# Attention: the first key block's product ahead of the third block's transposes, and where the projection passes stand

## The chip, the cores and the metric

The kernel runs on one core of a Trainium2 chip. The measured number is device time in microseconds (us) of one execution; smaller is better. The engines are TensorE (PE in the profile, its weight loads PEld), VectorE (DVE), ScalarE (ACT), GpSimd (POOL) and SyncE (SP, which issues the transfers).

## The reference, cut to what matters

One encoder layer over 1024 rows of width 1024. The mixing half has sliding-window attention (8 query heads, 2 key/value heads, blocks of 128 queries that see three blocks of 128 keys) beside a retention branch; both go through one output projection, and a gated feed-forward follows. The part that the change touches is the attention:

```python
s = einsum('bnqkgd,bnjkd->bnkgqj', qb, kb) * scale      # 128 queries x up to 3x128 keys
p = exp(s - m) / (sum(exp(s - m)) + exp(sink - m))      # m: row maximum, with the sink
o = einsum('bnkgqj,bnjkd->bnqkgd', p, vb)               # o: the product with the values
h = x + concat(o, retention) @ w_out
```

## The kernel before

Everything is float32. Each operand of a large product is split into a rounded part (hi, type fp32r) and the remainder (lo), and a product is three passes: hi by hi, hi by lo, lo by hi. A pass is one matmul of 128x512.

The attention stage is a loop of 16 steps (`for i in range(2 * NT)`, L782): query block t from 0 to 7, and key/value head kv 0 and 1. The generator `attend(t, kv, ...)` (L665) makes one step; its tiles are named after it, so `q40p` is a tile p of block 4, head 0. In it, four head rows j:

- scores: two matmuls for each j into a PSUM bank (`s`), then one VectorE instruction adds the mask and takes the extremum (`sm`, `nm`). `es` is a VectorE addition of 128x4 for the sink.
- ScalarE takes the exponentials (`sm`, sums into `den`). VectorE adds `es` to `den` and takes the reciprocal; then GpSimd and ScalarE, two rows each, scale `sm` (table entry `p_n`).
- transposes: for each key block b of nb (3; for t = 0 and 7 only 2), four 128x128 transposes of `sm` into a bank `p` on TensorE. ScalarE copies the bank to `ph` (hi), VectorE subtracts to `pl` (lo: bank `p` minus `ph`).
- product: for each b one matmul with `ph` and one with `pl` into bank `o`. ScalarE and VectorE add the two halves of `o` into `yA`.
- after head 1, GpSimd writes the block's rows to `X_hi` and `X_lo` (table entries `o_h`, `o_l`), from where the output projection reads them.

Transposes and products stand in two loops over b: all transposes first, then all products. `ph` has two buffers (tag t2), so the third `ph` is written once the first product has read the first. The banks come from five auxiliary ones (`AX_BUFS`), which the scores, the transposes and `o` share.

Beside these steps run, in the same loop, the queries of later blocks (`query`, tiles `q`, `q_t`, `qs`, `pt`, `qT`), the transposes of the retention rows (`ret_rows`, tiles `py`, `yw`), and projection passes that need nothing of the current step. `fill(n)` (L292) emits round(3n) passes from a fixed sequence, as long as their operands and a bank are there: first the rest of the query projection (tiles `d`), then the output projection (tiles `o`, whose weights `wh`, `wl` are split by GpSimd or ScalarE and VectorE on the way). The table `FILL` (L38) holds the counts; `fill(FILL["T1"])` at L699 emits 9 passes ahead of the transposes of each step.

The order of the code is not the order on the engines. A scheduler sorts each engine's instructions by readiness and priority as it computes them; program order decides between equals, and buffers set the waits. So a change of the emission order in `attend` changes the order on TensorE, and with it that of VectorE, ScalarE and GpSimd through the whole attention stage.

Of the kernel before, what the change touches and what calls it, by code (L numbers as in the profile page):

```python
# [34 lines left out]
       "r_bqh": "a", "r_bql": "ad", "r_sh": "a", "r_sl": "d", "r_y": "d", "r_sq": "a", "r_yn": "p", "r_yg": "p",  # L35
       "q_rope": "d", "k_rope": "d", "q_n": "d", "q_h": "p", "q_l": "dp", "q_T": "a", "p_n": "apap", "p_h": "a",
       "o_c": "a", "o_h": "p", "o_l": "p", "y_h": "a", "m_h": "da"}
FILL = {"A": 2, "Aend": 7, "B1": 2, "B2": 5, "C1": 4, "C2": 4, "D0": 6, "D1": 2, "T1": 3, "O0": 4, "O1": 4, "O2": 3}  # L38
SOONER = {"w": -80, "exp": 10, "pass": 0}
EARLY, LATE = (0, 4, 1, 5), (2, 3, 6, 7)  # L40
LEAD = 6
# [21 lines left out]
def hymba_block(ctx, tc, x, xT, cst, prm, ffnw, wqkv, wkv, wout, wg, wu, wd, out):  # L63
# [37 lines left out]
    def on(op, i=0):  # L101

        e = ENG[op]
        return {"a": act, "d": dve, "p": pool}[e[i % len(e)]]

    def copy(op, out, in_, i=0, scale=None):

        eng = on(op, i)
        if eng is act:
            act.activation(out, in_, AF.Copy, scale=1.0 if scale is None else scale)  # L110
        elif scale is not None:
            eng.tensor_scalar(out, in_, scale, 1.0, op0=ALU.mult, op1=ALU.mult)
        elif eng is dve:
            dve.tensor_copy(out, in_)
        else:
            pool.tensor_scalar(out, in_, 1.0, 1.0, op0=ALU.mult, op1=ALU.mult)
# [16 lines left out]
    def f32(ap):  # L133
        return ap.bitcast(F32)

    def U(name, tag, dt=F32):
        return up.tile([P, 512], dt, name=name, tag=tag, bufs=SLOTS[tag])
# [4 lines left out]
    def ax_ps(name):  # L142
        return pp.tile([P, 512], F32, name=name, tag="ax", bufs=AX_BUFS)
# [8 lines left out]
    def x_rows(t, k0):  # L152

        return tuple(X[:, k0:k0 + 4, t * P:t * P + P] for X in (X_hi, X_lo))

    def four(v):
        return v[:].rearrange("p (j n) -> p j n", n=P)
# [34 lines left out]
    A, B, C, D, O = "a", "b", "c", "d", "o"  # L192
# [57 lines left out]
    def sip():  # L250

        c, t, k = seq[pos[0]]
        per = 2 if c[0] == C else 1
        g = first_granule[c] + k // per
        i = part[0]
        if i == 0:
            while len(W) <= g:
                load_next()
            if c == chunks[0] and t == 0:
                split_x(k, 0)  # L260
            if k == 0:
                banks[c, t] = (ax_ps if c == chunks[0] and t in EXTRA else mm_ps)(f"{c[0]}{c[1]}_{t}")
                begun[0] += 1
        width = 512 // per
        o = (k % per) * width
        lh, ll = (X[:, k, t * P:t * P + P] for X in (X_hi, X_lo))
        rh, rl = (w[:, o:o + width] for w in W[g])
        with sooner("pass"):
            pe.matmul(banks[c, t][:, :width], ll if i == 2 else lh, rl if i == 1 else rh,
                      start=k == 0 and i == 0, stop=k == 7 and i == 2)  # L270
        part[0] = (i + 1) % 3
        if i < 2:
            return
        pos[0] += 1
        if c == chunks[0] and t == 3:
            split_x(k, 1)
        if k == 7:
            done.add((c, t))
        if t == tiles[c][-1] and (k + 1) % per == 0:
            freed[0] = g + 1  # L280
        if not hold[0] and pos[0] % PUMP == 0:
            pump(1)

    def ready():
        if pos[0] >= len(seq):
            return False
        c, t, k = seq[pos[0]]
        if (c[0], t, k // 4) in blocked:
            return False
        return k > 0 or part[0] > 0 or begun[0] - taken[0] < MM_BUFS + (len(EXTRA) if c == chunks[0] else 0)  # L290

    def fill(n):  # L292

        n = round(3 * n)
        while n and ready():
            sip()
            n -= 1
# [138 lines left out]
    def kv_scan(g, KV):  # L436
        gg = bc(gt[:, :, 2 * g:2 * g + 2], 3, HD)
        for s in range(1, 7):
            tmp = st.tile([P, 2, 2, HD], F32, name=f"sc{g}{s}", tag="sc", bufs=1)
            on("scan").tensor_tensor(tmp[:], KV(s - 1), gg, op=ALU.mult)  # L440
            on("scan").tensor_tensor(KV(s), KV(s), tmp[:], op=ALU.add)
# [83 lines left out]
    def drain(gen):  # L525
        for _ in gen:
            pass

    def go(gen):
        next(gen, None)  # L530
# [4 lines left out]
    for g in range(2):  # L535
# [4 lines left out]
        for t in range(NT):  # L540
# [9 lines left out]
            drain(prev)  # L550
            fill(FILL["A"])
            go(gen)
# [8 lines left out]
        drain(prev)  # L561
        fill(FILL["Aend"])
        kv_scan(g, KV)
        vhl = U(f"vhl{g}0", TAG["vhl"], F32R)
        states(g, 0, KV, BD, krv[0][:, 256:512], vhl)
        for c in range(NT):
# [6 lines left out]
            go(old)  # L573
            fill(FILL["B1"])
            go(gen)
            drain(old)
            fill(FILL["B2"])
            go(gen)
# [86 lines left out]
    def attend(t, kv, qT, yA):  # L665


        n = f"q{t}{kv}"
        b0 = max(t - 1, 0)
        nb = min(t + 1, NT - 1) - b0 + 1  # L670
        nk = nb * P
        mo = (b0 - (t - 1)) * P
        hs = slice(4 * kv, 4 * kv + 4)
        nm, es, den = (st.tile([P, 4], F32, name=f"{n}{v}", tag=v) for v in ("nm", "es", "den"))
        pr = []
        for j in range(4):
            pss = ax_ps(f"{n}s{j}")
            for i in range(2):
                pe.matmul(pss[:, :nk], qT[kv][:, j * P:j * P + P], K[:, 2 * kv + i, b0 * P:b0 * P + nk],
                          start=i == 0, stop=i == 1)  # L680
            sm = U(f"{n}sm{j}", "kr")
            dve.tensor_tensor_reduce(sm[:, :nk], pss[:, :nk], mask[:, mo:mo + nk], 1.0, 3.0e38, ALU.add, ALU.min,
                                     accum_out=nm[:, j:j + 1])
            pr.append(sm)
        dve.tensor_tensor(nm[:], nm[:], nsink[:, hs], op=ALU.min)
        dve.tensor_tensor(es[:], nm[:], sink[:, hs], op=ALU.add)
        yield
        for j in range(4):
            act.activation(pr[j][:, :nk], pr[j][:, :nk], AF.Exp, bias=nm[:, j:j + 1], scale=-1.0,
                           accum_out=den[:, j:j + 1])  # L690
            if j == 0:
                act.activation(es[:], es[:], AF.Exp)
        yield
        dve.tensor_tensor(den[:], den[:], es[:], op=ALU.add)
        dve.reciprocal(den[:], den[:])
        for j in range(4):
            copy("p_n", pr[j][:, :nk], pr[j][:, :nk], j, den[:, j:j + 1])
        yield
        fill(FILL["T1"])  # L699
        po = ax_ps(f"{n}o")  # L700
        ph, pl = [], []
        for b in range(nb):
            pt = ax_ps(f"{n}p{b}")
            for j in range(4):
                pe.transpose(pt[:, j * P:j * P + P], pr[j][:, b * P:b * P + P], f32(ident[:]))
            ph.append(U(f"{n}ph{b}", TAG["ph"], F32R))
            pl.append(U(f"{n}pl{b}", TAG["pl"], F32R))
            copy("p_h", ph[b][:], pt[:], b)
            dve.tensor_tensor(pl[b][:], pt[:], f32(ph[b][:]), op=ALU.subtract)
        for b in range(nb):  # L710
            vv = vview(b0 + b)[:, kv].rearrange("p i e -> p (i e)")
            pe.matmul(po[:], vv, ph[b][:], start=b == 0, stop=False)
            pe.matmul(po[:], vv, pl[b][:], start=False, stop=b == nb - 1)
        yield
        own = slice(kv * HD, kv * HD + HD)
        other = slice(HD - kv * HD, P - kv * HD)
        copy("o_c", yA[own, :], po[other, :])
        dve.tensor_tensor(yA[own, :], yA[own, :], po[own, :], op=ALU.add)
        if kv:
            yh, yl = x_rows(t, 0)  # L720
            copy("o_h", yh, four(yA))
            on("o_l").tensor_tensor(yl, four(yA), f32(yh), op=ALU.subtract)
            blocked.discard((O, t, 0))
# [14 lines left out]
    for t in range(NT):  # L738
# [6 lines left out]
        drain(old)  # L745
        fill(FILL["C1"])
        drain(prev)
# [171 lines left out]
    def prepare(n):  # L919

        for unit, v in order[prepared[0]:prepared[0] + n]:
            if v == "A11":
                for w in ("A11", "A12", "A21", "A22"):
                    block(unit, w)
            ready_ops[unit, v] = split(f"{v}_{unit[0]}{unit[1]}", block(unit, v))
        prepared[0] += n
# [6 lines left out]
    def product(ps, unit, v, xv, first, last):  # L933
        prepare(max(0, used[0] + 1 + LEAD - prepared[0]))
        used[0] += 1
        wh, wl = ready_ops[unit, v]
        xh, xl = XOP[xv]
        for k in range(4):
            c = slice(k * P, k * P + P)
            passes(ps[:], wh[:, c], wl[:, c], xh[:, k, :], xl[:, k, :], first and k == 0, last and k == 3,  # L940
                   skip_group_check=not first)
# [256 lines left out]
```

## Time and profile before

| what | value |
|---|---|
| time, median of 3 runs | 1137.11 us (1136.93 to 1137.37) |
| the profiled execution | 1136.94 us, its span 1135.2 us |
| TensorE busy | 1117.2 us, 98% of the span |
| VectorE, ScalarE, GpSimd busy | 815.0, 573.4, 164.8 us |
| attention loop in the trace | about 300 to 425 us after the start |

The span is the time from the first to the last instruction; 1.74 us of the profiled execution lie around it. A matmul's busy time overlaps that of the next one, so the pace of TensorE is read from start to start of its rows, not from their durations; a wait shows as a longer step from one start to the next.

### The profile page before, as it was taken

To read this page: it belongs to the slowest core of one execution; us is meant where nothing else is said; L and a number is where in the kernel's file an instruction comes from. 1 tells how busy PE (TensorE), PEld (TensorE's weight loads), DVE (VectorE), ACT (ScalarE), POOL (GpSimd) and SP (SyncE) were. 2 spreads that over 40 slices of the span, in tenths; PEclk is the share of its full clock that TensorE was granted. 3 is DMA by queue.
4 is the path that set the end of the run, shared out by engine and by line. 5 is a ranking of instruction groups with operands and counts; after the bars stand their busy time and mean duration, and the time that the engine had idled before them with its cause. 6 is when DMAs were issued, how large, how long until landed. Compare 5 with 4: busy or idle time off the path is not lost.

```text
span 1135.2 us, 16184 instructions
## 1 busy us (share of the span) xinstructions
PE 1117.2 (98%) x5384; PEld 925.6 (82%) x5384; DVE 815.0 (72%) x1647; ACT 573.4 (51%) x1196; POOL 164.8 (15%) x248
## 2 busy tenths in 40 slices
PE   9999999999999999999999999999999999999998
PEld 7777788789888778788888888888888888888887
DVE  6887857888799997879776577666766655555553
ACT  7954645554589785555333333333333334444441
POOL 1224400444455531000000000000000000000000
PEclk9999999999999999999999999999999999999999
DMA  8520202011100036733554356445544778766681
GB/s 327 183 57 1 75 1 75 1 56 39 38 1 10 20 101 212 240 96 112 176 195 148 114 183 194 141 120 185 188 138 129 261 229 261 248 212 195 218 267 65
DMA packets 84755, 156.53 MB, mean 138 GB/s; under 512 B 9664, under 2 KB 10176, under 8 KB 84672
## 3 DMA queue, kind: packets, MB, share of 16 engines
q1 hardware_dynamic: 84672, 155.51, 42.8%
q8 instruction: 42, 0.69, 0.3%
q14 instruction: 41, 0.34, 0.1%
HBM read 115.36 MB, written 40.11 MB: 137 GB/s over the span
## 4 chain that ended last, share of the span: by engine, by line
PE 83%; DVE 7%; ACT 3%; issue 3%; POOL 3%; DMA 0%; SPq 0%; POOLq 0%; ACTq 0%; DVEq 0%
PE pa L90 21%; PE pc L90 11%; PE da L90 10%; PE pb L90 5%; PE dc L90 5%; PE a L90 5%; PE b L90 5%; PE o L90 4%; PE d L90 3%; PE db L90 3%; PE c L90 1%; POOL Y L90 1%; DVE h L90 1%; ACT KV L90 1%; PE idle L90 0%
## 5 line engine op out<-in xcount | busy, mean ns | idle before, releaser
L90 PE MATMUL b<-wh,X_hi 128*128 128x512 f32 x128 | 51.5, 404 | 0.0
L90 PE MATMUL b<-wh,X_lo 128*128 128x512 f32 x128 | 51.0, 399 | 0.0
L90 PE MATMUL o<-wl,X_hi 128*128 128x512 f32 x128 | 50.4, 396 | 0.6 <-DVE wl L90 0.6
L90 PE MATMUL b<-wl,X_hi 128*128 128x512 f32 x128 | 50.8, 398 | 0.0
L90 PE MATMUL o<-wh,X_hi 128*128 128x512 f32 x128 | 50.7, 397 | 0.0
L90 PE MATMUL a<-wh,X_hi 128*128 128x512 f32 x128 | 50.4, 394 | 0.0
L90 PE MATMUL o<-wh,X_lo 128*128 128x512 f32 x128 | 50.1, 393 | 0.0
L90 PE MATMUL a<-wl,X_hi 128*128 128x512 f32 x128 | 50.0, 392 | 0.0
L90 PE MATMUL a<-wh,X_lo 128*128 128x512 f32 x128 | 49.7, 391 | 0.0
L90 DVE TENSOR_TENSOR S<-A,A 128x512 f32<-128x512 f32 x44 | 30.2, 686 | 1.7 <-DMA A<-in_wg_dram 1.2
L93 DVE TENSOR_TENSOR wl<-raw,wh 128x512 fp32r<-128x512 f32 x44 | 30.6, 711 | 0.1
L90 PEld LDWEIGHTS o<-wl,X_hi 128*128 128x128 f32 x128 | 24.1, 188 | 5.7 <-DVE wl L90 1.4
L90 ACT ACTIVATE sg<-sg 128x512 f32<-128x512 f32 x33 | 20.8, 632 | 15.4 <-DVE sg L90 15.4
L90 PEld LDWEIGHTS a<-wh,X_hi 128*128 128x128 f32 x128 | 24.2, 189 | 4.8
L90 PEld LDWEIGHTS b<-wh,X_lo 128*128 128x128 f32 x128 | 24.3, 190 | 4.6
L90 PEld LDWEIGHTS o<-wh,X_lo 128*128 128x128 f32 x128 | 24.1, 188 | 4.6
L90 PEld LDWEIGHTS b<-wl,X_hi 128*128 128x128 f32 x128 | 24.4, 190 | 4.1 <-DVE wl L93 0.2
L90 PEld LDWEIGHTS a<-wl,X_hi 128*128 128x128 f32 x128 | 24.2, 189 | 4.3
L90 PEld LDWEIGHTS a<-wh,X_lo 128*128 128x128 f32 x128 | 24.0, 188 | 4.4
L90 PEld LDWEIGHTS o<-wh,X_hi 128*128 128x128 f32 x128 | 24.1, 188 | 4.3
L90 DVE TENSOR_TENSOR wl<-raw,wh 128x512 fp32r<-128x512 f32 x32 | 22.0, 718 | 7.4 <-ACT wh L90 7.4
L90 PEld LDWEIGHTS b<-wh,X_hi 128*128 128x128 f32 x128 | 24.3, 190 | 3.6
(2925 smaller groups left out, 3745.5 us busy)
## 6 DMA issues: line engine op xcount, KB each, us to landing
A<-in_wg_dram SPq DMA_DIRECT2D x44, 256.0 KB, 2.8
A<-in_wu_dram SPq DMA_DIRECT2D x44, 256.0 KB, 3.1
R<-in_wd_dram SPq DMA_DIRECT2D x44, 256.0 KB, 2.7
L_S<-LS SPq DMA_DIRECT2D x44, 256.0 KB, 2.3
R_T<-RT SPq DMA_DIRECT2D x44, 256.0 KB, 2.1
raw<-in_wqkv_dram SPq DMA_DIRECT2D x40, 256.0 KB, 3.3
L_A<-a SPq DMA_DIRECT2D x33, 256.0 KB, 2.3
raw<-in_wout_dram SPq DMA_DIRECT2D x32, 256.0 KB, 2.9
```

What stands on the lines that cost most here:

```text
L90: ins = fn(*args, **kw)
L93: ins = fn(*args, **kw)
```

## The change

The table `FILL` gets three counts for a step instead of one: 2 passes (`T1`), 4 (`T2`) and 3 (`T3`), again 9 in all. The two loops over b become two functions, `turn` (transposes, `ph`, `pl` of one block) and `product` (the two matmuls of one block), and a step emits: 2 passes, transposes of blocks 0 and 1, 4 passes, product of block 0, transposes of block 2 if there is one, 3 passes, the other products.

```diff
-"T1": 3,
+"T1": 2 / 3, "T2": 4 / 3, "T3": 1,
...
-        fill(FILL["T1"])
         po = ax_ps(f"{n}o")
         ph, pl = [], []
-        for b in range(nb):
+        def turn(b):
             pt = ax_ps(f"{n}p{b}")
...
-        for b in range(nb):
+        def product(b):
             vv = vview(b0 + b)[:, kv].rearrange("p i e -> p (i e)")
...
+        fill(FILL["T1"])
+        turn(0)
+        turn(1)
+        fill(FILL["T2"])
+        product(0)
+        if nb == 3:
+            turn(2)
+        fill(FILL["T3"])
+        for b in range(1, nb):
+            product(b)
```

Both kernels have the same instructions on every engine (5384 matmuls). What moves is their order. On TensorE, the transposes and first products of block 2, head 0 (`q20p`: transposes, `q20o`: product, `q3pt`: transposes of a later query, `d`: passes), before:

```order
L93 MATMUL q20p_3997<-ident,q20sm_3888 128x128
L93 MATMUL q20p_4006<-ident,q20sm_3888 128x128
L93 MATMUL q20p_4015<-ident,q20sm_3883 128x128
L93 MATMUL q20p_4015<-ident,q20sm_3888 128x128
L90 MATMUL d_5_3986<-wh_3018,X_lo 128x512
L90 MATMUL d_5_3986<-wh_3033,X_hi 128x512
L90 MATMUL d_5_3986<-wl_3034,X_hi 128x512
L90 MATMUL d_5_3986<-wh_3033,X_lo 128x512
L93 MATMUL q20o<-q20ph_4002,V_2969 128x512
L90 MATMUL q3pt_4035<-ident,q3qs_3943 128x128 x4
L90 MATMUL d_5_3986<-wh_3328,X_hi 128x512
L90 MATMUL d_5_3986<-wl_3329,X_hi 128x512
```

and now:

```order
L93 MATMUL q20p_3999<-ident,q20sm_3888 128x128
L90 MATMUL d_5_3987<-wl_3329,X_hi 128x512
L90 MATMUL d_5_3987<-wh_3328,X_lo 128x512
L90 MATMUL d_5_3987<-wh_3351,X_hi 128x512
L93 MATMUL q20o<-q20ph_3995,V_2969 128x512
L93 MATMUL q20p_4014<-ident,q20sm_3873 128x128
L93 MATMUL q20p_4014<-ident,q20sm_3878 128x128
L93 MATMUL q20p_4014<-ident,q20sm_3883 128x128
L93 MATMUL q20p_4014<-ident,q20sm_3888 128x128
L90 MATMUL q3pt_4035<-ident,q3qs_3943 128x128 x4
L90 MATMUL d_5_3987<-wl_3352,X_hi 128x512
L93 MATMUL q20o<-q20pl_3996,V_2969 128x512
```

The third block's four transposes went from in front of the passes to behind the first product, and three passes instead of four stand between. On VectorE, around the remainders `q70pl` of block 7, head 0 (`q6yA`: the result of block 6, `h`: residual rows, `yw`: retention rows), before:

```order
L90 TENSOR_TENSOR q6yA<-q6yA,q61o 64x512
L90 TENSOR_TENSOR q71nm<-q71nm,nsink 128x4
L90 TENSOR_TENSOR h_5195<-o_0_4640,xr_5194 128x512
L90 TENSOR_TENSOR q71es<-q71nm,prmt 128x4
L93 TENSOR_TENSOR q70pl_5092<-q70p_5086,q70ph_5091 128x512
L93 TENSOR_TENSOR q70pl_5101<-q70p_5095,q70ph_5100 128x512
```

and now:

```order
L90 TENSOR_TENSOR q6yA<-q6yA,q61o 64x512
L93 TENSOR_TENSOR q70pl_5085<-q70p_5079,q70ph_5084 128x512
L93 TENSOR_TENSOR q70pl_5094<-q70p_5088,q70ph_5093 128x512
L90 TENSOR_TENSOR q71nm<-q71nm,nsink 128x4
L90 TENSOR_TENSOR yw_5124<-py_5119,idx 128x512
L90 TENSOR_TENSOR q71es<-q71nm,prmt 128x4
```

`q71es` went from ahead of the two remainders to behind them; `q61es` of block 6 likewise went behind all three `q60pl` (before, it stood between the first and the second). On VectorE, ahead of the remainders of block 4, head 0 (`wl`: remainder of projection weights, `q6q`, `q_t`: a later query), before:

```order
L90 TENSOR_TENSOR q41es<-q41nm,prmt 128x4
L93 TENSOR_TENSOR wl_4483<-raw_4481,wh_4482 128x512
L90 TENSOR_TENSOR q6q<-d_6_4190,cosT 128x512
L93 TENSOR_TENSOR q40pl_4411<-q40p_4405,q40ph_4410 128x512
L93 TENSOR_TENSOR q40pl_4420<-q40p_4414,q40ph_4419 128x512
```

and now:

```order
L90 TENSOR_TENSOR q3yA<-q3yA,q31o 64x512
L90 TENSOR_TENSOR q_t_4460<-d_6_4191,sinT 128x512
L93 TENSOR_TENSOR wl_4483<-raw_4481,wh_4482 128x512
L90 TENSOR_TENSOR q6q<-q6q,q_t_4460 128x512
L93 TENSOR_TENSOR wl_4489<-raw_4487,wh_4488 128x512
L93 TENSOR_TENSOR q40pl_4404<-q40p_4398,q40ph_4403 128x512
```

The second weight remainder, `wl_4489`, came forward from block 5 to a place ahead of block 4's remainders.

## Rows read from the trace of the kernel before

**Rows 1.** The profile's page: busy times, and the chain that ended last by engine.

```profile
PE 1117.2 (98%) x5384; PEld 925.6 (82%) x5384; DVE 815.0 (72%) x1647; ACT 573.4 (51%) x1196; POOL 164.8 (15%) x248
...
PE 83%; DVE 7%; ACT 3%; issue 3%; POOL 3%; DMA 0%; SPq 0%; POOLq 0%; ACTq 0%; DVEq 0%
```

**Rows 2.** Busy times by stretch: stretch, length, engines' busy us (instructions), PE clock, DMA.

```profile
323.93:366.87 42.94, 42.91 (x245) 35.73 (x244) 39.59 (x115) 39.10 (x102) 23.24 (x36) 1.00 0.00 1
366.87:392.78 25.91, 24.45 (x142) 20.19 (x141) 24.72 (x63) 20.33 (x49) 17.52 (x22) 1.00 0.08 22
392.78:424.57 31.79, 31.11 (x174) 24.96 (x172) 29.31 (x75) 26.06 (x71) 10.95 (x15) 1.00 0.30 92
```

**Rows 3.** TensorE's waits from 300 to 425 us: total us, times, longest.

```profile
PE q50o L93 <- DVE q50pl L93: 0.8, 1, 0.8
PE q51s L90 <- DVE yw L90: 0.4, 1, 0.4
PE q70o L93 <- DVE q70pl L93: 0.4, 1, 0.4
PE q60o L93 <- DVE q60pl L93: 0.3, 1, 0.3
```

**Rows 4.** TensorE in order of time: start, us, operation, idle before; transposes and passes.

```profile
321.74 1.47 PE L93 MATMUL q10p<-ident,q10sm 128*128 128x128 f32 x12
322.96 0.48 PE L90 MATMUL d<-wh,X_hi 128*128 128x512 f32 x1
323.28 0.39 PE L90 MATMUL d<-wl,X_hi 128*128 128x512 f32 x1
323.51 0.39 PE L90 MATMUL d<-wh,X_lo 128*128 128x512 f32 x1
...
342.86 0.66 PE L93 MATMUL q21p<-ident,q21sm 128*128 128x128 f32 x4
343.27 0.48 PE L90 MATMUL d<-wl,X_hi 128*128 128x512 f32 x1
343.59 1.04 PE L93 MATMUL q21p<-ident,q21sm 128*128 128x128 f32 x8
344.38 0.48 PE L90 MATMUL d<-wh,X_lo 128*128 128x512 f32 x1
```

**Rows 5.** The same view: a first product, block 1, head 1.

```profile
330.17 0.48 PE L90 MATMUL d<-wh,X_hi 128*128 128x512 f32 x1
330.55 0.50 PE L93 MATMUL q11o<-q11ph,V 128*128 128x512 f32 x1
330.89 0.51 PE L90 MATMUL q21s<-K,q2qT 128*128 128x384 f32 x2
```

**Rows 6.** The same view, VectorE beside GpSimd at four places.

```profile
366.87 1.28 DVE L93 TENSOR_TENSOR q40pl<-q40p,q40ph 128x512 fp32r<-128x512 f32 x2
366.93 1.28 POOL L90 TENSOR_TENSOR X_lo<-q3yA,X_hi 128x512 fp32r<-128x512 f32 x1
...
383.45 1.29 POOL L90 TENSOR_TENSOR X_lo<-q4yA,X_hi 128x512 fp32r<-128x512 f32 x1
383.49 1.27 DVE L90 TENSOR_TENSOR q51es<-q51nm,prmt 128x4 f32<-128x4 f32 x1
...
401.95 1.27 DVE L90 TENSOR_TENSOR q61es<-q61nm,prmt 128x4 f32<-128x4 f32 x1
...
417.15 1.27 DVE L90 TENSOR_TENSOR q71es<-q71nm,prmt 128x4 f32<-128x4 f32 x1
```

**Rows 7.** The same view: short VectorE operations alone, and beside GpSimd's weight copies.

```profile
364.48 1.21 POOL L93 TENSOR_SCALAR wh<-raw 128x512 fp32r<-128x512 f32 x2
...
365.05 0.15 DVE L90 TENSOR_TENSOR q41es<-q41nm,prmt 128x4 f32<-128x4 f32 x1
365.14 1.09 DVE L93 TENSOR_TENSOR wl<-raw,wh 128x512 fp32r<-128x512 f32 x1
...
377.83 0.61 DVE L90 TENSOR_TENSOR q6qs<-q6q,q6qs 128x256 fp32r<-128x256 f32 x1 [0.88 <-POOL q6qs L90]
```

More of the change, by code (lines that the diff above doesn't have):

```diff
@@ L37 @@
        "o_c": "a", "o_h": "p", "o_l": "p", "y_h": "a", "m_h": "da"}
-FILL = {"A": 2, "Aend": 7, "B1": 2, "B2": 5, "C1": 4, "C2": 4, "D0": 6, "D1": 2, "T1": 3, "O0": 4, "O1": 4, "O2": 3}
+FILL = {"A": 2, "Aend": 7, "B1": 2, "B2": 5, "C1": 4, "C2": 4, "D0": 6, "D1": 2, "T1": 2 / 3, "T2": 4 / 3, "T3": 1, "O0": 4, "O1": 4, "O2": 3}
 SOONER = {"w": -80, "exp": 10, "pass": 0}
```

## The prediction

> **What bounds the kernel now.** I read the page first, then busy times by stretch, then TensorE's waits, then the engines in order of time around each wait. The page [rows 1] shows TensorE at 98% of the span, and the chain that ended last runs over it for 83%. So an edit that adds no work can bring no more than TensorE's waits, and costs what waits it adds. The edit lies in the attention loop, 300 to 425 us. There the stretches [rows 2] show something the page hides: VectorE is nearly as full as TensorE. From the first `q40pl` to the first `q51pl` (366.87 to 392.78) it is busy 24.72 of 25.91 us, and TensorE's clock is at 1.00, its 2.4 GHz level, in all three stretches. VectorE is in the path of every product: it makes `pl` from `ph`, and the product waits for it.
>
> TensorE's waits [rows 3] are four that the profile names, 1.9 us together; three of them are for a remainder `pl`, one for a bank that VectorE frees (`yw`). Behind a wait the next matmul comes 0.34 us later instead of 0.23 (330.55 to 330.89) [rows 5], so each wait costs 0.11 more: 2.3 us for the four. Some eight first products have a short wait besides: in rows 5 the pass takes 0.38 from start to start (330.17 to 330.55), where 0.32 is the step behind transposes (322.96 to 323.28) [rows 4], so 0.06 and then 0.11; 1.4 us for eight. All that could be won is about 3.7 us. 0.2%, or 2.3 us, is about what a measurement of this kernel can tell from no change.
>
> Why are the remainders late? In three places (383.49, 401.95, 417.15) [rows 6] a VectorE addition of 128x4, `es`, takes 1.27 us; alone it takes 0.15 [rows 7]. The first of them started 0.04 us behind GpSimd's `X_lo` of 1.29 us and ended with it. Each stands directly ahead of, or between, the `pl` that TensorE then waits for: `q50pl`, `q60pl`, `q70pl` are the three names of rows 3. The `pl` themselves are not held: at 366.87 two of them took 1.28, 0.64 each, while GpSimd ran an `X_lo` from 366.93. `pl` has one operand in PSUM; `es` has both in SBUF.
>
> The Trainium skill, page SBUF — State Buffer, section Who interferes with whom, says the same as a rule: a VectorE instruction with two SBUF inputs and a GpSimd instruction that reads SBUF exclude each other, and the later one is blocked in full. The rows agree, 1.27 against 0.15. By that rule a `wl`, a sum of two SBUF tiles, can be held as `es` is, which speaks against this change where it puts more `wl` ahead of remainders; that result is the second rival below.
>
> **The change part by part.** *Work.* Every engine has the same instructions, so nothing is added. Splitting the transposes makes 44 stints of them in the stage instead of 31 (counted in the order from the first score to the feed-forward's first transposes). The price from rows 4: twelve in one stint take 1.22 (321.74 to 322.96); four and eight take 0.41 and 0.79, 1.20 together, and each stint makes its next pass 0.32 instead of 0.23. So a stint costs 0.09 - 0.02 = 0.07 at most, as the 0.41 holds a wait too, and 0.02 below zero to nothing if the short last transpose pays for it. 13 more: 0 to +0.9; I take +0.3, nearer to zero for the wait in it.
>
> *The first product.* From the last transpose of block 0 to its product the order has three passes instead of four or five (two in block 1, head 1), but the third block's four transposes no longer stand between. The path through ScalarE's `ph` is as long as before. Three passes are 0.32 + 2 x 0.23 = 0.78 where one sufficed for a wait of 0.06 in rows 5 with four transposes beside it (0.41). So the short waits stay as they are: 0, with -1.4 if all go and +1.0 if eight double.
>
> *The third block.* Its `ph` could not be written before the first product anyway (two buffers), and now its transposes run beside that wait. Between the first `ph` and the first `pl` product the order now has four transposes (0.41) and one to four short ones of a query. Cost 0 as long as VectorE is prompt: 0.64 for a `pl` against 0.23 + 0.41.
>
> *The `es` that hold `pl` up.* The order on VectorE now has `q61es` behind all three `q60pl` and `q71es` behind both `q70pl`; what GpSimd holds there no longer stands in front of the product. Removed: 0.3 + 0.4 + 2 x 0.11 = 0.9. Late next is the weights' `wl` behind `q61es`, read by passes that stand behind the last `q60` product. Bounds 0 and -0.9; I take -0.9. `q51es` now follows `q4yA` at once, before GpSimd can start `X_lo` (which needs `q4yA` and a copy first), but a `wl` and a reduction stand between it and `q50pl`. One is traded for the other: 0, from -0.9 (0.8 + 0.11) to +0.6.
>
> *The bank at `q51s`.* In the old order VectorE waited 0.88 for GpSimd's `q6qs` [rows 7], ahead of `yw`, because GpSimd's weight copies waited for the last query passes. These passes now all stand ahead of `q40`'s first product, so the copies come sooner relative to it. Removed: 0.4 + 0.11 = 0.5; bounds 0 and -0.5; I take -0.5.
>
> *Block 4.* Ahead of `q40pl` stand now two `wl` and `q6q`. One `wl` more is 0.6, one held as in rows 7 is 1.09 + 0.11 = 1.2. TensorE arrives there as late as before. Bounds 0 and +1.2; I take +0.6, the unheld one.
>
> *Passes that move.* Counted in the order, 77 passes instead of 60 stand between the first products of `q10` and `q40`, 23 instead of 36 between `q40` and `q51`, 59 instead of 62 from there to `q71`. As work this cancels. As cover it doesn't: 13 x 0.23 = 3.0 us of passes are missing in the very stretch where VectorE is 95% full. TensorE is busy for 24.45 of the 25.91 there and idle for 1.46 [rows 2]; without the 13 passes it needs 21.5. VectorE has 57 rows there instead of 62: a `q_t`, a query sum, a `yA` and a mask step fewer, one `wl` more, so three large ones of 0.6, and 24.72 - 1.8 = 22.9 is left, 24.1 with its idle time of 1.2. So VectorE sets this stretch now, and TensorE is idle in it for 1.4 to 2.6 us, as long as before or 1.2 longer. Bounds 0 and +1.2; I take 0, because a hold of 1.1 and the wait of 0.88 for `q6qs` are in VectorE's 25.91 and were counted above. The first stretch takes 3.9 us more passes with VectorE at 92% as before.
>
> Sum: +0.3 + 0 + 0 - 0.9 + 0 - 0.5 + 0.6 + 0 = -0.5 us. Against the profiled execution, 1136.94 (span 1135.2 and 1.74 around it), that is 1136.4; the median shown is 0.17 above it. Forecast 1136.4.
>
> **The rivals.** *All long waits go* (faster): the holds fall on nothing that TensorE waits for, and `wl` are in time. -2.3 for the four, -1.4 for the short ones: 1136.94 - 3.7 = 1133.2. For it: two of the three `es` are behind their `pl` now. Against it: VectorE's 95% leaves little to give.
>
> *The thinned stretch* (slower): GpSimd's copies or `X_lo` hold a `wl` or a query sum in blocks 3 and 4, ahead of `q30pl`, `q40pl` and `q50pl`, and the passes that would have covered it have been spent. It decides as soon as TensorE reaches the first `pl` product earlier than VectorE by more than the transposes there. Three such holds at 1.2 and 1.2 more in the thinned stretch, with 0.3 for the stints and less the 0.9 and 0.5 won: 3.6 + 1.2 + 0.3 - 1.4 = +3.7, or 1140.6. For it: 13 passes fewer, and block 4's projection passes, which need GpSimd's `X_hi` of block 4, now stand ahead of `q50`'s first product. Against: VectorE has fewer operations in the same stretch.
>
> *It doesn't do what it says*: the scheduler, not the code, places passes (fewer than two stand ahead of most transposes' ends, three behind), and the new waits equal the old: 1136.9, within the forecast's case.
>
> **How the numbers follow.** Forecast with the neutral rival 0.57, its own range 1134.8 to 1139.4, which is 2.3 us on either side of the median and holds the sum with any two terms at their bounds; all waits go 0.27; thinned stretch 0.16. These are also the chances of within 0.2%, faster and slower, since the two rivals end outside 2.3 us. The range has to reach the first rival and the milder half of the second (one or two holds): 1133.0 to 1139.7 leaves out about 0.09 on either side.
>
> **What would show it.** In the changed trace: no wait named `q60o` or `q70o` for a `pl` (right for the `es`); `q61es` and `q71es` may still take 1.27. `q51s` not waiting for `yw`. The length from the first `q40pl` to the first `q51pl`: under 23.5 if VectorE's holds are gone, over 24.5 for the thinned stretch. From the first `q10` to the first `q40pl` it should be 46 to 47 us. A new wait at `q30o` or `q40o` beside a VectorE row far over 0.7 would be the second rival. Wrong altogether would be a change in the stretches after 430 us, which I take as untouched.

## The result: 5.4 us slower, 1142.37 against 1136.93 us

The changed kernel takes 1142.37 us (median of 5 runs, 1141.73 to 1144.11), the kernel before 1136.93 in the same series: a ratio of 1.0051, 95% interval 1.0039 to 1.0062. The forecast was 1136.4, its range 1133.0 to 1139.7. So it is slower, and it lies 2.7 us above the upper end of the range.

The profiled execution took 1142.92 us, 5.98 more than that of before, and its span is 1141.1 instead of 1135.2. The page after, as in [rows 1] busy times and the chain by engine:

```profile
PE 1118.7 (98%) x5384; PEld 924.7 (81%) x5384; DVE 816.6 (72%) x1647; ACT 574.7 (50%) x1196; POOL 167.2 (15%) x248
...
PE 80%; DVE 8%; issue 4%; POOL 4%; ACT 3%; DMA 1%; SPq 0%; POOLq 0%; DVEq 0%; ACTq 0%
```

The work is the same. What shrank is TensorE's share of the chain, from 83% to 80%: it waits. TensorE's waits after, from 300 to 436 us (total, times, longest), against [rows 3]:

```profile
PE q40p L93 <- POOL q40sm L90: 2.1, 1, 2.1
PE q50p L93 <- ACT q50sm L90: 1.0, 1, 1.0
PE q31p L93 <- DVE q40nm L90: 1.0, 1, 1.0
PE q21p L93 <- DVE q30nm L90: 0.4, 1, 0.4
PE q71p L93 <- POOL q71sm L90: 0.3, 1, 0.3
PE q30p L93 <- POOL q30sm L90: 0.2, 1, 0.2
PE q71p L93 <- ACT q71sm L90: 0.2, 1, 0.2
```

None of the four names of [rows 3] is left: no product waits for a `pl` and no score for `yw`. All the new names end in `p`. TensorE now waits in front of the *transposes*, for the scaled probabilities `sm` or for a bank, 5.2 us instead of 1.9.

The three stretches of [rows 2], from first `pl` to first `pl` on VectorE (`q10` to `q40`, to `q51`, to `q71`), after: length, then busy time and instructions of TensorE, its weight loads, VectorE, ScalarE, GpSimd, then TensorE's clock and the transfers:

```profile
323.40:374.01 50.61, 46.91 (x258) 38.26 (x257) 44.05 (x118) 41.17 (x105) 29.36 (x41) 1.00 0.04 10
374.01:396.86 22.85, 21.69 (x130) 17.86 (x129) 21.98 (x57) 19.50 (x46) 13.88 (x17) 1.00 0.13 39
396.86:428.86 32.00, 31.44 (x176) 24.80 (x173) 29.22 (x76) 26.23 (x70) 11.21 (x15) 1.00 0.23 75
```

The first is 7.67 longer than before; 17 more passes there are 3.9 of it, and 3.8 are waits. The second is 3.06 shorter, as much as its 13 missing passes (3.0). The third is 0.2 longer with three passes fewer (0.7), but not by waits: TensorE is idle there for 0.56 us, before for 0.68 [rows 2], and it has four transposes more in it. The start of the first stretch lies 0.5 earlier, and 1.6 are added behind the last one: -0.5 + 7.7 - 3.1 + 0.2 + 1.6 = 5.9.

**Where the largest wait comes from.** GpSimd after, in order of time, at block 4 (start, us, operation):

```profile
366.24 1.98 POOL L93 TENSOR_SCALAR wh<-raw 128x512 fp32r<-128x512 f32 x3 [6.26 <-PE d L90]
368.20 0.31 POOL L90 TENSOR_SCALAR q6a<-q6a,e 128x8 f32<-128x8 f32 x1
368.59 1.64 POOL L90 TENSOR_TENSOR q6b<-q6a,mhalf 128x8 f32<-128x8 f32 x1
370.20 0.68 POOL L93 TENSOR_SCALAR wh<-raw 128x512 fp32r<-128x512 f32 x1
370.87 2.09 POOL L90 TENSOR_SCALAR q40sm<-q40sm,q40den 128x384 f32<-128x384 f32 x2
```

VectorE and TensorE at the same place:

```profile
368.15 0.17 DVE L90 RECIPROCAL q40den<-q40den 128x4 f32<-128x4 f32 x1
...
370.32 1.10 DVE L90 TENSOR_TENSOR q6q<-q6q,q_t 128x512 f32<-128x512 f32 x1
371.34 0.68 DVE L93 TENSOR_TENSOR wl<-raw,wh 128x512 fp32r<-128x512 f32 x1
```

```profile
370.08 0.27 PE L93 MATMUL q40p<-ident,q40sm 128*128 128x128 f32 x1
372.45 1.00 PE L93 MATMUL q40p<-ident,q40sm 128*128 128x128 f32 x7 [2.10 <-POOL q40sm L90]
```

The factor for block 4's rows was there at 368.32. GpSimd took them up at 370.87, 2.55 later, because its queue had `q6a`, `q6b` and a weight copy ahead of them. It then needed 2.09 for two rows, where the pair of `q31sm` took 1.17 (below). One row of `q40p` was transposed at 370.08; the next had to wait until 372.45. Before, GpSimd sat idle until the factor came (363.17), began 0.19 later, and all twelve transposes ran in one piece:

```profile
363.00 0.17 DVE L90 RECIPROCAL q40den<-q40den 128x4 f32<-128x4 f32 x1
363.36 1.16 POOL L90 TENSOR_SCALAR q40sm<-q40sm,q40den 128x384 f32<-128x384 f32 x2 [5.20 <-DVE q40den L90]
364.20 1.47 PE L93 MATMUL q40p<-ident,q40sm 128*128 128x128 f32 x12
```

**A second place.** VectorE's waits after, and GpSimd ahead of them, at block 3:

```profile
359.43 0.82 DVE L90 TENSOR_TENSOR q5qs<-q5q,q5qs 128x256 fp32r<-128x256 f32 x1 [1.78 <-POOL q5qs L90]
360.17 0.54 DVE L90 CUSTOM_DVE_ANT_0 q40sm<-q40s,mask 128x384 f32<-128x384 f32 x1
```

```profile
357.13 0.74 POOL L90 TENSOR_TENSOR q5qs<-q5q,q5qs 128x256 fp32r<-128x256 f32 x1
357.85 1.17 POOL L90 TENSOR_SCALAR q31sm<-q31sm,q31den 128x384 f32<-128x384 f32 x2
358.98 0.41 POOL L90 TENSOR_SCALAR q5qs<-q5q 128x256 fp32r<-128x256 f32 x1
```

VectorE stands 1.78 us in front of `q5qs`, a remainder of a *later* query. The scores `q40s` begin during that wait, and their masks are behind `q5qs` in the queue. TensorE's rows after, and then the scores and the first mask before:

```profile
358.30 1.51 PE L90 MATMUL q40s<-K,q4qT 128*128 128x384 f32 x7
360.78 1.14 PE L93 MATMUL q31p<-ident,q31sm 128*128 128x128 f32 x8 [0.97 <-DVE q40nm L90]
```

```profile
355.35 1.56 PE L90 MATMUL q40s<-K,q4qT 128*128 128x384 f32 x8
355.90 0.56 DVE L90 CUSTOM_DVE_ANT_0 q40sm<-q40s,mask 128x384 f32<-128x384 f32 x1 [0.46 <-PE q40s L90]
```

Before, the first mask came 0.55 behind the first score, and VectorE waited for it; now it comes 1.87 behind (358.30 to 360.17). So not all of the 1.78 is lost, but 1.3 of delay is, the run of `q5qs` itself included. The banks of these scores are what `q31p` then waits 1.0 us for. The Trainium skill, page TensorE: Matmul & The Clock Gate, section Architectural detail: the array is 16× 32×32, not 1× 128×128, says that VectorE's queue is strictly first in, first out; these rows agree.

### The profile page after: what moved, and what is told of

Same layout as the page of the kernel before. It is cut to its first block, busy times and chain, and to the rows that moved or that the text cites. A ratio compares the mean times of both kernels' runs of the same rounds, so it can differ in the third digit from the quotient of the medians.

```text
span 1141.1 us, 16178 instructions
## 1 busy us (share of the span) xinstructions
PE 1118.7 (98%) x5384; PEld 924.7 (81%) x5384; DVE 816.6 (72%) x1647; ACT 574.7 (50%) x1196; POOL 167.2 (15%) x248
## 4 chain that ended last, share of the span: by engine, by line
PE 80%; DVE 8%; issue 4%; POOL 4%; ACT 3%; DMA 1%; SPq 0%; POOLq 0%; DVEq 0%; ACTq 0%
PE pa L90 21%; PE pc L90 10%; PE da L90 10%; PE pb L90 5%; PE dc L90 5%; PE a L90 5%; PE o L90 5%; PE b L90 4%; PE db L90 3%; PE d L90 3%; PE c L90 1%; POOL Y L90 1%; DMA xr<-in_x_dram 0%; DVE h L90 0%; PE idle L90 0%
```

## The experiments

Each run has its own median of before in its series (1136.3 to 1137.0). The table has the number of projection passes that the order of each kernel puts ahead of the first transposes of `q20`, `q30` and `q40`, counted from the first transposes of the step before; the length of the trace from the first `q10p` to the first `q50p`, with TensorE's instructions in it as recorded; what of that length is not passes (length - 58.96 - 0.23 for each instruction beyond 332; some records are missing, so good to some tenths); and the medians.

| kernel | passes ahead | length (matmuls) | beyond passes | median - before | ratio, 95% |
|---|---|---|---|---|---|
| before | 12, 12, 13 | 58.96 (332) | 0 | | |
| changed | 17, 21, 21 | 66.26 (343) | +4.8 | +5.4 | 1.0039 to 1.0062 |
| e1 reorder alone | 12, 12, 13 | 58.89 (333) | -0.3 | +1.4 | 1.0005 to 1.0023 |
| e2 passes alone | 17, 21, 12 | 65.55 (344) | +3.8 | +4.5 | 1.0025 to 1.0052 |
| e3 scaling first | 17, 21, 12 | 63.87 (340) | +3.1 | +5.6 | 1.0036 to 1.0061 |
| e4 six ahead | 12, 12, 13 | 60.18 (334) | +0.8 | +3.1 | 1.0017 to 1.0037 |
| e5 blocks 5 to 7 | 12, 12, 13 | 58.99 (332) | 0.0 | +2.2 | 1.0012 to 1.0030 |
| e6 blocks 0 to 4 | 17, 21, 21 | 66.30 (343) | +4.8 | +5.8 | 1.0040 to 1.0066 |
| e7 `q40` on ScalarE | 17, 21, 21 | 66.68 (349) | +3.8 | +4.1 | 1.0030 to 1.0055 |
| e8 head 0 alone | 12, 12, 13 | 58.96 (334) | -0.5 | +1.7 | 1.0003 to 1.0021 |
| e9 head 1 alone | 17, 21, 12 | 65.47 (343) | +4.0 | +6.3 | 1.0039 to 1.0065 |
| e10 power behind | 17, 22, 19 | 70.01 (347) | +7.6 | +8.6 | 1.0064 to 1.0090 |
| e11 `q50` alone | 12, 12, 13 | 58.98 (332) | 0.0 | +0.1 | 0.9991 to 1.0009 |

Up to `q50p` the table parts in two. The five experiments with 12, 12 and 13 passes ahead are within 0.8 us of before. The changed kernel and the six with 17 and 21 (or 22) ahead lose 3 to 8 us there, whatever else differs. The medians part less cleanly: four of the five are still 1.4 to 3.1 us above before, by what happens behind `q50p`. Only e11, which moves one step, is level with it.

**The two parts of the change (e1, e2).**

```diff
 e1: -"T1": 2 / 3, "T2": 4 / 3, "T3": 1,
     +"T1": 3, "T2": 0, "T3": 0,
 e2:          turn(1)
     +        if nb == 3:
     +            turn(2)
              fill(FILL["T2"])
              product(0)
     -        if nb == 3:
     -            turn(2)
              fill(FILL["T3"])
```

> The first product ahead of the third block's transposes, as in the changed kernel, but all 9 passes stay ahead of the transposes (counts 9, 0, 0). In its order of instructions as many passes stand between the first transposes of one step and the next as in the kernel before (12 ahead of q20p, 12 ahead of q30p, 13 ahead of q40p), GpSimd has one weight copy ahead of the scaling of q40sm instead of none, and VectorE's es stand where they stood. Theory A (the loss comes from where the passes went: GpSimd's and VectorE's work of the next softmax is late for the transposes): 1136.5 to 1138, waits q50o and q60o for pl still there, no wait of q40p for the scaling above 0.5 us. Rival B (the loss comes from the reorder itself: more stints of transposes, a third ph and pl later): 1140 to 1142.

> The other part alone: 2 passes ahead of the transposes, all transposes of a step in one piece, then 4 passes, the first product, 3 passes, the other products. In the order 17 passes stand ahead of q20p and 21 ahead of q30p, as in the changed kernel, but 12 ahead of q40p instead of 21, and GpSimd scales q40sm ahead of q6a and q6b, behind four weight copies that come earlier. Theory A: slower than before, but without the wait of 2.1 us at q40p: 1138.5 to 1140.5, with waits of q30p or q31p for the scaling or for a bank. Rival B: 1136 to 1138, no new waits at the transposes.

Measured: 1138.14 and 1141.24 us, 0.1 and 0.7 above theory A's ranges, far from rival B's. The reorder costs 1.4, none of it up to `q50p`; the passes carry the loss. e2 has no long wait at `q40p`, and loses as much; its waits are elsewhere:

```profile
PE q30o L93 <- DVE q30pl L93: 1.1, 1, 1.1
PE q50p L93 <- ACT q50sm L90: 0.9, 1, 0.9
PE q21p L93 <- DVE q30nm L90: 0.7, 1, 0.7
```

**How many passes behind the transposes (e4).** One line: `"T1": 6 / 3, "T2": 2 / 3, "T3": 1 / 3`.

> The changed kernel with the nine passes split 6, 2, 1 instead of 2, 4, 3. In the order 12, 12 and 13 passes stand ahead of q20p, q30p and q40p as before, 17, 13 and 17 ahead of q50p, q51p and q60p, and one weight copy of GpSimd is ahead of the scaling of q40sm. Theory A: the number of passes behind the transposes decides; with three of nine the scheduler keeps the old places and the time is 1136 to 1138. Rival B (the reorder itself costs): 1140 to 1142.

Measured: 1139.85. The counts up to `q40` stay and so, nearly, does the time up to `q50p` (+0.8, of which 0.6 is a wait of `q51s` for `yw`, 1.0 instead of 0.4). But the total is nearly 2 us above theory A's range and close to rival B's: behind `q50p` it waits 0.8 each at `q50o` and `q70o`. So theory A is right on the place and doesn't cover the whole.

**Which heads and which blocks (e8, e9; e5, e6).** A condition `split` (head 0, head 1, t >= 5, t < 5) chooses for each step between the new and the old form:

```diff
-        fill(FILL["T1"])
+        split = kv == 0
+        fill(FILL["T1"] if split else 3)
         turn(0)
         turn(1)
-        fill(FILL["T2"])
-        product(0)
+        if split:
+            fill(FILL["T2"])
+            product(0)
...
-        for b in range(1, nb):
+        for b in range(1 if split else 0, nb):
```

> The new order in the steps of head 0 alone; the steps of head 1 keep 9 passes ahead and all transposes before the products. In the order the counts ahead of q20p to q50p are those of before (12, 8, 12, 8, 13, 8, 15), and the es of blocks 5 to 7 stand behind the pl. Theory A (the passes behind head 1's transposes are what goes ahead of the next head 0's): 1135 to 1137, no new wait at the transposes of blocks 2 to 5. Rival B (reorder and split cost wherever they stand): 1138.5 to 1140.5, about half of the loss.

> The complement of the run with head 0 alone: the new order in the steps of head 1, the steps of head 0 as before. In the order 17, 21 and 12 passes stand ahead of q20p, q30p and q40p (before 12, 12, 13), and GpSimd has q5a and q5b ahead of the scaling of q30sm. Theory A (head 1's seven passes behind its transposes land ahead of the next head 0's transposes, where they bring the work of a later query ahead of the softmax): +3.5 to +5.5, 1140.5 to 1142.5, with waits at q31p or q30o and at q50p, though not 2 us at q40p. Rival B (both heads' steps cost alike): +1 to +2.5, like head 0.

> The new order (2 passes, transposes, 4 passes, product, transposes, 3 passes, products) for the steps of blocks 5 to 7 alone; blocks 0 to 4 as in the kernel before. In its order the counts of passes ahead of q20p to q50p are those of before, and the es of blocks 5, 6 and 7 stand behind all pl. Theory A (the loss is made in blocks 2 to 4, where the passes of head 1's step go ahead of the next head 0's transposes; the part after that gains what was predicted): no wait of q50o, q60o, q70o for pl, none of q40p: 1135 to 1136.5, at or below before. Rival D (whatever is moved, waits of 3 to 5 us come back elsewhere): 1138 to 1140.

> The reverse: the new order for blocks 0 to 4 alone, blocks 5 to 7 as before. The counts ahead of q20p to q50p and GpSimd's order (five weight copies, q6a and q6b ahead of the scaling of q40sm) are those of the changed kernel. Theory A: the waits of q31p, q40p and q50p are there as in the changed kernel, with q60o and q70o besides: 1141 to 1143. Rival D: no clear place, 1138 to 1141.

Measured: head 0 alone 1138.64, head 1 alone 1143.24; blocks 5 to 7 alone 1139.2, blocks 0 to 4 alone 1142.79. Only the last lies in theory A's range. Head 1 alone is 0.7 above it, and head 0 alone is 1.6 above it, at the lower end of rival B's. Up to `q50p` the whole loss is in head 1's steps of the early blocks. The seven passes that stood ahead of head 1's transposes stand behind them now, and there they are the first thing TensorE can do while the next head 0's softmax runs: 12 become 17 and 21. The same split in head 0's steps moves none of these counts. The rows of the stretch from the first `q10p` to the first `q50p` (columns as in the stretches above), of the kernel with head 0 alone, and then of that with head 1 alone:

```profile
321.41:380.37 58.96, 58.65 (x334) 48.34 (x333) 55.91 (x153) 53.32 (x135) 35.97 (x53) 1.00 0.02 6
```

```profile
321.87:387.34 65.47, 62.14 (x343) 50.09 (x342) 57.70 (x158) 53.26 (x135) 37.04 (x52) 1.00 0.05 13
```

What head 0's split and the late blocks cost, 1.7 and 2.2, lies behind `q50p`. For blocks 5 to 7, theory A missed by nearly 3 us, and rival D's range holds: the waits of `q60o` and `q70o` for `pl` do go, but `q70s` waits 1.0 for `yw` and `q51p` 0.4 for its scaling instead (head 0 alone has the same two). What the `es` give is taken back beside them. Nor do the pieces add up: the two heads alone cost 8.0 together, the early and the late blocks 8.0, and the whole change 5.4.

**The smallest piece (e11).** The new form in block 5, head 0, and nowhere else.

> The new order in one step alone, block 5, head 0. VectorE's q51es then stands behind all three q50pl; TensorE's order differs in 30 rows, all behind q50p. Theory A: the wait of 0.8 us at q50o shrinks to 0.4 or less, and 14 passes instead of 17 ahead of q51p bring a wait of 0.4 there: 1136.3 to 1137.3, not to be told from before. Rival D (any change of order costs 1 to 2 us): 1138 to 1139.

Measured: 1137.00 against 1136.93, no difference, as theory A had it. Its waits show the trade in one step:

```profile
PE q51p L93 <- POOL q51sm L90: 0.5, 1, 0.5
...
PE q50o L93 <- DVE q50pl L93: 0.3, 1, 0.3
```

`q50o` fell from 0.8 to 0.3 as `q51es` went behind the `pl`, and `q51p` came with 0.5.

**Taking single holds away (e3, e7, e10).** The three edits to the changed kernel: priority 10 for the step that scales; ScalarE for all four rows of `q40sm`; GpSimd's scalings and powers held to the order of the code.

```diff
 e3:  +        with sooner("sc"):
      +            go(nxt)
 e7:  -            copy("p_n", ..., j, den[:, j:j + 1])
      +            copy("p_n", ..., 0 if n == "q40" else j, den[:, j:j + 1])
 e10: +            pinned[0] = j % 2 == 1
                   copy("p_n", ..., j, den[:, j:j + 1])
 ...
      +        pinned[0] = True
               pool.tensor_scalar(a[:], a[:], e2[:, t:t + 1], 1.0, ...)
               pool.tensor_tensor(b[:], a[:], mhalf[:], op=ALU.pow)
```

> The changed kernel, with priority 10 for the step that adds den, takes the reciprocal and scales the probabilities (the priority that the step of transposes and products has already). In the order GpSimd now scales q40sm ahead of q6a and q6b, and 12 passes instead of 21 stand ahead of q40p; ahead of q20p and q30p it is still 17 and 21. Theory A (GpSimd's queue holds the scaling): the wait of 2.1 us at q40p goes, most of 2.3 us: 1139.5 to 1140.5. Rival C (the wait at q40p is set by the later scores and exponentials of q40, not by GpSimd's queue): the wait moves to ScalarE's half or to the exponentials, 1141.5 to 1143.

> The changed kernel with all four rows of q40sm scaled by ScalarE, the other steps as they were. Up to q40p the counts of passes are the same (17, 21, 4, 21), GpSimd still has its weight copies, q6a and q6b there, but nothing of q40p waits behind them. Two scalings more on ScalarE take 1.1 us. Theory A1 (GpSimd's queue is what q40p waits for): the wait of 2.1 us shrinks to 1.3 or less, and q40p's excess of 2.3 with it; what comes of the total depends on whether the cover is missing further on: 1140.5 to 1142. Rival C (q40p waits for the late softmax whatever engine scales): the wait at q40p stays at 2 us or more.

> The changed kernel, with GpSimd held to the order of the code for the scalings and for the two steps of a query's power, so that q20sm, q30sm and q40sm are scaled ahead of q4a/q4b, q5a/q5b and q6a/q6b. The passes ahead of q20p, q30p and q40p are 17, 22 and 19, as in the changed kernel (17, 21, 21). Theory A1 (GpSimd's queue holds the scaling, and that is the loss): the excess of 0.35 at q30p goes and that of 2.3 at q40p falls under 1; 1139 to 1140.5. Theory A2 (the queue is only where the lateness shows; the loss is that the passes are spent ahead of q30p and q40p and lacking as cover later): the waits move to pl products, to banks or to q50p, and the time stays at 1141 to 1143.

Measured: 1142.33, 1141.07, 1145.48. In all three the wait of `q40p` for GpSimd is gone. e3 got nothing for it, as rival C had it: `q50p` waits 1.1, `q50o` 0.6 for `ph`, and a pass 0.7 for `wl`. e7 gained 1.3 against the changed kernel, though their intervals overlap, and put a wait of 1.3 at `q40o` for its `pl`; it lies in theory A1's range. e10 is the worst of all and outside both ranges, with GpSimd in the very order that theory A1 wanted:

```profile
PE q21p L93 <- DVE q30nm L90: 1.9, 1, 1.9
PE q40o L93 <- DVE q40pl L93: 1.8, 1, 1.8
PE q50p L93 <- ACT q50sm L90: 1.1, 1, 1.1
```

The power comes late there, so a query comes late, VectorE stands 2.7 us in front of `q4q`, and the masks behind it are late. Of its 7.6 beyond the passes some 3.4 are TensorE's clock, which fell twice (last section); the 4.2 that remain are within what the others lose. That GpSimd's order at `q40sm` is the loss, as I had read it from the trace, is refuted: it is where the lateness showed.

**Which link (e12 with e13, e14 with e15).** Two edits, each made to the changed kernel and to the one before, so that the difference between the orders is read with the support work altered. e12 and e13 leave out the normalisation of the queries. e14 and e15 put both remainders of a query on GpSimd and the rounding of this stage's weights on ScalarE, so that no such remainder or `wl` on VectorE waits for GpSimd.

```diff
 e12, e13: -        dve.tensor_reduce(a[:], q32[:]..., AX.X, ALU.add)
 ...
           -        pool.tensor_scalar(a[:], a[:], e2[:, t:t + 1], ...)
           -        pool.tensor_tensor(b[:], a[:], mhalf[:], op=ALU.pow)
 ...
           -        on("q_n").tensor_tensor(q3, q3, bc(b[:], 2, HD), op=ALU.mult)
 e14, e15: -W_HOLD = "pd"
           +W_HOLD = "ad"
           -"q_l": "dp"
           +"q_l": "pp"
```

> The changed kernel without the normalisation of the queries: for each block VectorE's sum of squares and its product with the factor, and GpSimd's two steps of the power, are left out (VectorE 1.2 us and GpSimd 1.9 us less for each block; TensorE's work is the same). In the order 22, 21 and 17 passes stand ahead of q20p, q30p and q40p. To be read against the old order with the same left out. Theory S (the passes ahead of head 0's transposes cost because the query's work on VectorE and GpSimd comes ahead of the softmax with them): with that work halved the difference between new and old order falls from 5.4 to 2 us or less, and the waits at q31p, q40p and q50p nearly go. Theory A2 (the passes are spent too early and lacking as cover, whatever the other engines have to do): the difference stays at 4 to 6 us.

> The kernel before without the normalisation of the queries, the control of the run beside it. In the order 13, 11 and 10 passes stand ahead of q20p, q30p and q40p. Both theories: 1133 to 1136.5, since TensorE's waits there are 2.3 us in all and its work is the same; what counts is the difference to the run beside it (theory S: 2 us or less; theory A2: 4 to 6 us).

> The changed kernel, with both query remainders on GpSimd (VectorE makes none) and the rounded weights of this stage on ScalarE instead of GpSimd. So no wl and no query remainder on VectorE waits for GpSimd any more; 21, 21 and 21 passes stand ahead of q20p, q30p and q40p. To be read against the old order with the same edit. Theory V (the passes pulled ahead put operations that wait for GpSimd into VectorE's queue in front of the softmax and the pl): the waits of VectorE for GpSimd of 0.9 to 1.8 us go, and new minus old falls from 5.4 to 2 us or less. Theory A2 (the passes are spent ahead of the transposes while the softmax takes as long as it takes, and are lacking later): 4 to 6 us.

> The kernel before with the same edit, the control; 13, 12 and 13 passes ahead of q20p, q30p and q40p. Both theories: 1135 to 1139; GpSimd has one subtraction of 0.7 us more for each block, ScalarE some eleven copies of 0.6 more and GpSimd as many fewer. What counts is the difference to the run beside it (theory V: 2 us or less; theory A2: 4 to 6 us).

| pair | new order | old order | difference, 95% | beyond passes, `q10p` to `q50p`, new and old |
|---|---|---|---|---|
| as they are | 1142.37 (+5.4) | 1136.93 | 5.4 (4.7 to 7.2) | 4.8 and 0 |
| without the normalisation | 1141.78 (+5.5) | 1138.08 (+1.8) | 3.7 (2.8 to 6.1) | 3.1 and -0.5 |
| no VectorE operation of a query's remainder or a `wl` behind GpSimd | 1140.68 (+3.8) | 1138.44 (+1.6) | 2.2 (1.4 to 2.9) | 2.6 and 1.1 |

In brackets behind a time stands its distance from before in its series; the intervals are worked out by redrawing at random from the runs of each pair. No pair fell into a theory's range: 3.7 lies between the two, 2.2 just above theory V's. And in both pairs the control moved: the old order, expected at 1133 to 1136.5 in e13, lost 1.8 there and 1.6 in e15.

So less support work does not shrink the loss by what the medians show: the new order is as far from before without the normalisation (5.5) as with it (5.4), and the two intervals overlap. Up to `q50p` alone the new order loses less, 3.1 instead of 4.8. VectorE is busy for only 54.90 of 65.27 us in that stretch of e12, and still late:

```profile
355.91 1.20 DVE L93 TENSOR_TENSOR wl<-raw,wh 128x512 fp32r<-128x512 f32 x1 [3.33 <-POOL wh L93]
357.14 1.29 DVE L93 TENSOR_TENSOR q30pl<-q30p,q30ph 128x512 fp32r<-128x512 f32 x2
```

```profile
352.93 0.61 POOL L90 TENSOR_SCALAR X_hi<-q2yA 128x512 fp32r<-128x512 f32 x1
353.62 1.29 POOL L90 TENSOR_TENSOR X_lo<-q2yA,X_hi 128x512 fp32r<-128x512 f32 x1
354.89 0.41 POOL L90 TENSOR_SCALAR q5qs<-q5q 128x256 fp32r<-128x256 f32 x1
355.26 0.62 POOL L93 TENSOR_SCALAR wh<-raw 128x512 fp32r<-128x512 f32 x1
```

A `wl` stands in VectorE's queue ahead of `q30pl` and waits 3.33 for a `wh` that GpSimd makes behind its own scaling, `X_hi`, `X_lo` and a query. It is the picture of the changed kernel's 1.78 at `q5qs`, with another operation at the head. In the stretch from `q10p` to `q50p`, VectorE waits for GpSimd for 2.7 to 4.6 us in each of the seven kernels that lose there, and for 0.3 to 0.9 in before and the five that don't. In the changed kernel it is 2.7:

```profile
DVE q5qs L90 <- POOL q5qs L90: 1.8, 1, 1.8
DVE q4qs L90 <- POOL q4qs L90: 0.9, 1, 0.9
```

In e14 none is left. Against before, the new order gains 1.6 by that edit (2.2 up to `q50p`, less 0.6 behind it); the other half of the smaller difference is the old order's loss. And the edit does more: eight weight copies of the attention loop go from GpSimd, the engine that is late, to ScalarE, seven remainders of queries from VectorE to GpSimd, and the order moves too (21, 21, 21 against 13, 12, 13 passes ahead). So the link through VectorE's queue is made likely, and not shown by itself. The sizes don't follow from it either: e2 and e9 wait 4.6 us and lose 3.8 and 4.0, the changed kernel waits 2.7 and loses 4.8, and e14 has no such wait and loses 2.6.

A second link runs beside it: passes spent early are lacking later as cover, that is, as work for TensorE while the softmax runs. The seven have 11 or 12 passes ahead of `q50p`, and it waits 0.8 to 1.1 in each; before and the five have 15 or 17, and it doesn't wait. In e15, with 14, it waits 0.3; in e14, with 7, the first of these:

```profile
PE q50p L93 <- ACT q50sm L90: 1.7, 1, 1.7
...
PE q40p L93 <- POOL q40sm L90: 0.7, 1, 0.7
```

So lacking cover fits about 1 us of the loss. But ScalarE has the weight copies in e14, and TensorE's clock fell there (below). No run changes cover alone, or that queue alone, so how the loss divides between the two stays open.

**A version that beats both** did not come out: e11 is level with before, every other order slower.

## Why the prediction was wrong, step by step

- *The `es` holds, -0.9*: right. In the changed kernel `q61es` and `q71es` follow their `pl` and take 0.15, and `q60o` and `q70o` don't wait. (The 0.15 that the prediction calls alone, at 365.05, lies beside a weight copy of GpSimd, begun at 364.48; `q40es` before, at 359.09 with GpSimd idle, takes 0.15 as well.) *The bank at `q51s`, -0.5*: right, that wait is gone. *`q51es`, 0*: `q50o` doesn't wait for `pl` any more, so -0.9, its lower bound; `q50p` waits 1.0 instead.
- *Stints, +0.3 (0 to +0.9), and the first product, 0 (-1.4 to +1.0)*: not measured apart. The reorder alone costs 1.4 us in all (0.6 to 2.6), above the 0.3 I took and inside the two bounds together, and nothing up to `q50p`.
- *Block 4, +0.6*: no wait for `q40pl` shows; the wait there is that of `q40p`, 2.1.
- *Passes that move, 0 (0 to +1.2)*: the step that failed. The stretch from which passes are missing behaved as worked out: under 23.5 was asked, 22.85 measured. I had bounded that one and dismissed the other in half a sentence, "the first stretch takes 3.9 us more passes with VectorE at 92% as before". It takes 3.9 for the passes and 3.8 more (46 to 47 us were forecast from `q10` to `q40`, 50.61 measured). I costed the passes where they had been and not where they went: ahead of head 0's transposes they bring a later query's operations and weight remainders forward in VectorE's and GpSimd's queues, in front of the softmax. VectorE there was busy for 44.05 us instead of 39.59 [rows 2] and idle for 6.6 instead of 3.4. That these passes, in head 1's early steps, carry the loss is shown (e1, e2, e8, e9); by which wait most of it comes is open (e14).
- *What I followed*: on VectorE the rows ahead of a `pl`, on GpSimd what holds one VectorE instruction beside it. I did not follow the path that ends at the transposes (mask, exponential, `den`, factor, scaling), though the change puts seven passes fewer in front of it.
- *All long waits go, 1133.2, chance 0.27*: the four named waits did go, and seven others came, 5.2 us in all instead of 1.9.
- *The second rival, 1140.6, chance 0.16*: right on the side, on the blocks (3 and 4) and on the engine that is late; wrong on the wait (transposes and a bank, not `pl`), on the mechanism as far as the rows show it (VectorE waits for a *result* of GpSimd; at the largest wait, 2.1, the blocking of one by the other makes 0.9, and there it is GpSimd that is held) and on the size, 1.8 us too small.
- *A change after 430 us, which would be "wrong altogether"*: there is one of 1.6 us in the profiled execution. TensorE waits 0.3 for `h` and 1.2 for a `wl`, where it waited 0.6 before, so 0.9 of it are waits. The first of it follows a transfer: `xr` was issued at 438.22 and `h` could start at 443.93, 5.7 later; before, 433.69 and 438.01, 4.3. The issues just ahead on SyncE's queue are the same in both, three weight tiles and one of `h`.

```profile
438.22 1.34 SPq L826 DMA_DIRECT2D xr<-in_x_dram  x3
...
443.93 0.69 DVE L90 TENSOR_TENSOR h<-o,xr 128x512 f32<-128x512 f32 x1 [4.82 <-DMA xr<-in_x_dram]
```

In the other traces it is 4.1 (e4) to 5.8 (e2), and 5.8 also with the reorder alone. Whether the change causes any of it is open; it is in one execution, and the medians differ by 0.5 less than the two profiled ones.

## What to carry over

When filler work changes its place, cost it at the place it goes to: list what the filler's *completion* makes ready on the other engines, and what of theirs it then stands ahead of. A wait that a trace names is the last link: three runs that removed the longest one gained 0, 1.3 and -3.1 us. The run that took operations waiting for a slow engine out of a busy engine's queue gained 1.6 of 5.4. Where an edit is made to two kernels so that their difference can be read, show both ends: here the control lost 1.8 and 1.6 us by the edit, and the difference alone hides that. And a term of zero needs bounds as much as any other, on both of the stretches between which something moves.

## What the hardware showed beyond that

GpSimd is slowed beside VectorE as VectorE is beside GpSimd: two scalings of `q40sm` took 2.09 us, 0.92 more than the pair of `q31sm` (1.17) a little earlier, while VectorE ran `q6q` (1.10) and `wl` (0.68), each on two SBUF operands. The prediction had only the other direction. The Trainium skill, page SBUF — State Buffer, section Who interferes with whom, says that the order of issue decides which of the two is held; these rows agree that it can be either.

TensorE's clock fell behind short waits, though not behind all. In e10 it waited 1.9 us at `q21p` and 1.82 for `q40pl`. The granted clock was 1.00 up to each and lower behind it: 0.67 in 5.2 us and 0.60 in 4.3, means of its two levels of 2.4 and 1.2 GHz:

```profile
347.40:352.60 5.20, 5.19 (x22) 4.39 (x23) 4.34 (x13) 1.88 (x4) 1.08 (x2) 0.67 0.00 0
...
376.00:378.70 2.70, 0.92 (x9) 0.74 (x7) 2.70 (x4) 1.16 (x4) 1.54 (x1) 1.00 0.38 97
378.70:383.00 4.30, 4.26 (x17) 3.67 (x18) 3.35 (x8) 2.07 (x4) 1.50 (x4) 0.60 0.33 83
```

In e14 it was 0.57 from 387.4 to 391.0, behind the waits of 1.7 and 0.6. In the changed kernel the wait of 2.1 at `q40p` left it at 1.00. Such a stretch costs about as much again as the wait: 5.2 x 0.33 = 1.7 and 4.3 x 0.4 = 1.7 us in e10, 3.6 x 0.43 = 1.5 in e14, an estimate from these rows. So some 3.4 us of what e10 lost, and 1.5 of what e14 lost in the profiled execution, is that.
